# Turning the first block of a down projection with VectorE and GpSimd copies instead of TensorE

## The chip, the cores and the metric

The kernel runs on one core of one Trainium2 chip. A core has a matrix engine (TensorE, PE in the profile, with its weight loads as PEld), a vector engine (VectorE, DVE), a scalar engine (ScalarE, ACT), a general engine (GpSimd, POOL) and a queue engine that issues most loads (SyncE, SP). The metric is the device time of one execution in microseconds (us).

## The reference

A decoder trunk of two layers on 256 tokens of width 2048 in float32. Layer 0 mixes the tokens with gated linear attention, layer 1 with block-sparse attention; after each comes a convolutional feed-forward part:

```python
def conv_ffn(x, norm_w, w_up, conv_w, conv_b, w_down):
    h = rms_norm(x, norm_w) @ w_up
    hp = jnp.pad(h, ((0, 0), (CONV_WIDTH - 1, 0), (0, 0)))
    acc = conv_b
    for j in range(CONV_WIDTH):
        acc = acc + conv_w[j] * hp[:, j:j + S]
    a, u = jnp.split(acc, 2, axis=-1)
    return (jax.nn.silu(a) * u) @ w_down
```

and in the trunk `h = h + conv_ffn(h, ...)`. The hidden width is 5632. The change touches the end of layer 0's feed-forward: the product with `w_down`, its addition to `h`, and the first part of the norm that follows.

## The kernel before

*Layouts.* The residual `h` is kept with features on the 128 partitions and tokens along the free dimension: eight tiles `h[0]` to `h[7]`, each 128 x 2 x 256 (256 features). Two of them share one slot (`hs[m]`). The down projection's products come out the other way round, tokens on the partitions and features along the free dimension, so its result has to be turned before it is added to `h`.

*Precision.* A float32 product is made of three products of a reduced type: each weight tile of 1024 columns is split into `whi` (ACT copies, line 144) and `wlo` (DVE subtracts, line 146), and each activation likewise. Four buffers each hold `whi` and `wlo`. Raw weights come into three buffers `wraw` by DMAs on SP's queue, in a fixed order.

*The down projection* (`down`, line 766) works in two blocks of 1024 output features. A block goes through 22 pairs of hidden tiles (`hid[0]` to `hid[21]`) in an order that is written out by hand (`ORDERS`). For plain pairs it does 24 matmuls; for pairs marked `+` or `^` a Strassen-like scheme with seven products does 21, and uses sums of weights that were made earlier, parked in DRAM (`tsum`) and loaded back, for `+` into two buffers named `ahead`, for `^` into two slots named `sums`. Block 1 of layer 0 has the order `0 2 4 6 1+ 3+ 5+ 7+ 9+ 11+ 13+ 18 15^ 14+ 16+ 17^ 19+ 12^ 10+ 8^ 20 21`: four plain pairs, then almost only pairs with seven products. At the start of pair number i the jobs of entry i in a table are issued first; before pairs 8 and 10 of block 1 these include two combinations of hidden tiles (DVE and ACT work).

*Slots.* Large tiles (4 KB per partition) come from one pool of 32 slots, `slot(...)`. The 22 hidden tiles, the combinations (`comb`, 10 slots by the end of block 0), the tiles of `h` when loaded back, the norm's operands (`xw`) and the `sums` tiles all come from it. A tile whose slot is not free waits for the last reader of the old one.

*The work around the change* (`first_down`, line 902). Block 0 ends with four tiles of sums, 128 tokens x 512 features each (`blocks[0]`: two halves of the features, `c`, times two halves of the tokens, `t`). During block 1, for each quarter q from 0 to 3 of that block, `back(q, in_acc)` makes four TensorE transposes (line 921, against an identity) into half of a PSUM tile of the accumulators' pool, and DVE adds that to `h[q]` (line 923). `load_back(m)` (line 925) brings two tiles of `h` from DRAM, where they were parked, by DMAs on POOL's queue. `nrm.feed(q)` makes the next norm's operand (ACT line 258, DVE line 262) and its squares (ACT lines 269 and 272, DVE line 273). The second block's quarters, 4 to 7, are turned after block 1 by `last_back`, with TensorE into other PSUM banks.

*What sets the order.* Instructions are issued in program order by priority, but the order on each engine is laid out at compile time by a planner that goes by its own costs and by when data and buffers come free; each engine then works through its queue in order. `after_low()` keeps a DVE instruction behind the latest subtraction of weights (line 146) that was issued before it, `after_high()` the same on ACT.

*The turning by squares* exists already: in the up projection (`turn_up`, lines 720 and 722) DVE transposes all 32 x 32 squares of a 128 x 512 tile in place of each other (`V.transpose`), and `square` (line 705) moves the squares to their partitions with 16 POOL copies of 32 x 256 elements.

Of the kernel before, what the change touches and what calls it, by code (L numbers as in the profile page):

```python
# [8 lines left out]
F32 = mybir.dt.float32  # L9
# [9 lines left out]
S = 256  # L19
# [139 lines left out]
def trunk(ctx: ExitStack, tc: tile.TileContext, xT, cst, msk, w1p, w2a, w_k, w_qa, w_v2, w_v, w_g, w_go,  # L159
          w_up0, w_dn0, w_kk, w_kv, w_mq, w_mo, w_up1, w_dn1, rel, onehot, out):  # L160
    nc = tc.nc
    V, A, T = nc.vector, nc.scalar, nc.tensor
# [7 lines left out]
    acc_ps = ctx.enter_context(tc.tile_pool(name="acc_ps", bufs=3, space=PSUM))  # L170
# [3 lines left out]
    def slot(shape, dt, name):  # L174
        return big.tile(shape, dt, name=name, tag="slot")

    def temp(name, shape=(128, 2, S), dt=F32):
        return tmp.tile(list(shape), dt, name=name, tag="temp")

    def bank(name, shape):  # L180
        return mis_ps.tile(list(shape), F32, name=name, tag="bank")
# [6 lines left out]
    for layer, todo in enumerate(ahead):  # L188
        t = dram.tile([len(todo), 128, 2048], F32, name=f"tsum{layer}")
# [15 lines left out]
    h = [hs[p // 2][:, p % 2] for p in range(NP)]  # L205
# [44 lines left out]
    def col(c):  # L250
        return gn[:, c - C_GN:c - C_GN + 1] if C_GN <= c < C_GN + KT else cs[:, c:c + 1]
# [69 lines left out]
    def after(steps, job):  # L321
        later.append((cur[0] + steps, job))
# [21 lines left out]
    def after_high():  # L344
        return tc.issue_after(ws.high.ins)

    def after_low():
        return tc.issue_after(ws.low.ins)
# [40 lines left out]
    def rows(xs):  # L389
        return lambda kt: xs[kt // 2][:, kt % 2, :]  # L390

    def both(ps, name):
        t = temp(name)
        A.copy(t, ps[:, :, S:])
        V.tensor_add(t, t, ps[:, :, :S])
        return t
# [8 lines left out]
    def split(dst_hi, dst_lo, src):  # L405
        A.copy(dst_hi, src)
        V.tensor_sub(dst_lo, src, dst_hi.bitcast(F32))
# [23 lines left out]
    nrm = Norm(C_GN, "xw", columns=True)  # L431
# [12 lines left out]
    xs = rows(nrm.xs)  # L444
# [92 lines left out]
    for hd in range(GH):  # L537
# [4 lines left out]
        b = bcum[hd]  # L542
# [64 lines left out]
    for hd in range(GH):  # L607
        ps = gemm(xs, KT)
        q = both(ps, "q")
# [60 lines left out]
    def combine(k, hid_k, halves_, kept=True):  # L670

        own = room(k, hid_k, kept) if k not in combos else rooms_of[k]
        t = sums(halves_)
        if own is not None and not kept:
            return split(own[:, :, 0], own[:, :, 1], t)
        if own is not None:
            split(own[:, 0:3, 0], own[:, 0:3, 1], t[:, 0:3])
        else:
            for f in range(3):
                split(*combos[k][f], t[:, f])  # L680
        split(*combos[k][3], t[:, 3])
# [18 lines left out]
    def square(y, x):  # L700

        for m in range(4):
            xs_ = x[32 * m:32 * m + 32].rearrange("a t (n c b) -> a n t c b", c=4, b=32)
            for c in range(4):
                nc.gpsimd.tensor_copy(y[32 * c:32 * c + 32, :, :, 32 * m:32 * m + 32], xs_[:, :, :, c])  # L705

    def ffn(layer, nrm, then):
        xs = rows(nrm.xs)
        hid = []
        combos.clear()  # L710
        cw = C_CW + layer * 3 * 2 * FT
        cb = C_CB + layer * 2 * FT

        def turn_up(g, ps):

            x = slot([128, 2, 512], F32, "uT")
            us = [temp("up", (128, 512)) for _ in range(2)]
            for t in range(2):
                with after_high():
                    A.activation(us[t], ps[:, t, :], AF.Copy, scale=nrm.col[:, t:t + 1])  # L720
                with after_low():
                    V.transpose(x[:, t], us[t])  # L722
            y = slot([128, 2, 2, S], F32, "up")
            square(y.rearrange("p j i (t s) -> p (j i) t s", t=2), x)
            for jj in range(2):
                after(UP_LAG[jj], lambda jj=jj: conv(g, jj, y[:, jj]))

        def conv(g, jj, t):

            j = 2 * g + jj  # L730
            au = temp("au")
            for i in range(2):
                n = i * FT + j
                with after_high():
                    A.activation(au[:, i, :], t[:, i, :], AF.Identity, bias=col(cb + n),  # L735
                                 scale=col(cw + 2 * 2 * FT + n))
            for i in range(2):
                n = i * FT + j
                with after_low():
                    V.scalar_tensor_tensor(au[:, i, 1:], t[:, i, :S - 1], col(cw + 2 * FT + n), au[:, i, 1:],  # L740
                                           op0=OP.mult, op1=OP.add)
                V.scalar_tensor_tensor(au[:, i, 2:], t[:, i, :S - 2], col(cw + n), au[:, i, 2:],  # L742
                                       op0=OP.mult, op1=OP.add)
            after(1, lambda: gate(g, jj, au))

        def gate(g, jj, au):
            with after_high():
                A.activation(au[:, 0, :], au[:, 0, :], AF.Silu)
            with after_low():
                V.tensor_mul(au[:, 0, :], au[:, 0, :], au[:, 1, :])  # L750
            if jj == 0:
                hid.append(slot([128, 2, 2 * S], F32R, "hid"))
            split(hid[g][:, jj, :S], hid[g][:, jj, S:], au[:, 0, :])
            whole[jj] = (au[:, 0, :128], au[:, 0, 128:])
            if jj and (g in EARLY or g in ASIDE):
                two = [whole[0], whole[1]]
                after(1, lambda: combine(g, hid[g], two) if g in EARLY else put_aside(layer, g, hid[g], two))

        whole = {}

        for g in range(FT // 2):
            ps = gemm_tok(xs)
            after(0, lambda g=g, ps=ps: turn_up(g, ps))
        then(hid)
# [137 lines left out]
    def first_down(hid, nrm):  # L902
        blocks = {}

        def ready(b, p):
            blocks[b] = r = u_sums(p, None)

            def end(c, ns):
                for t, n in enumerate(ns):
                    V.tensor_add(r[2 * t + c], r[2 * t + c], p[n])  # L910

            return end

        def back(q, where):

            r = blocks[q // 4]
            tp = where()
            c, i0 = q % 4 // 2, q % 2 * 2
            for i in range(2):
                for t in range(2):  # L920
                    T.transpose(tp[:, i, 128 * t:128 * t + 128],
                                r[2 * t + c][:, 128 * (i0 + i):128 * (i0 + i) + 128], ident)
            V.tensor_add(h[q], h[q], tp)

        def load_back(m):
            hs[m] = slot([128, 2, 2, S], F32, "h")
            for q in (2 * m, 2 * m + 1):
                h[q] = hs[m][:, q % 2]
                nc.gpsimd.dma_start(h[q], hspill[q].rearrange("a (b c) -> a b c", b=2))

        pair = []

        def in_acc():
            if not pair:
                two = acc_ps.tile([128, 2, 512], F32, name="acc")
                pair.extend(two[:, i].rearrange("p (a b) -> p a b", a=2) for i in range(2))
            return pair.pop(0)

        jobs = {}
        for i, job, n in ((0, load_back, 0), (0, load_back, 1), (2, back, 0), (2, back, 1), (3, back, 2), (3, back, 3),  # L940
                          (4, nrm.feed, 0), (6, nrm.feed, 1), (8, nrm.feed, 2), (10, nrm.feed, 3),
                          (15, load_back, 2), (16, load_back, 3)):
            jobs.setdefault(i, []).append(lambda job=job, n=n: job(n, in_acc) if job is back else job(n))
        down(0, hid, ready, {1: jobs})

        def last_back(q):
            back(q, lambda: bank("hf", (128, 2, S)))
            nrm.feed(q)

        for q in range(4, NP):  # L950
            after(q - 3, lambda q=q: last_back(q))
        after(5, nrm.close)
# [3 lines left out]
    for p in range(NP):  # L956
        after(6 + 2 * p, lambda p=p: park(p))
    n_q = Norm(C_MN, "xw", rows=False, columns=True)
    ffn(0, n_ffn, lambda hid: first_down(hid, n_q))


# [79 lines left out]
    def turn(hd):  # L1041

        t = slot([128, 2, 384], F32, "pT")
        with tc.issue_after(ws.low.ins):
            V.transpose(t[:, 0], pts[hd])
        to = turned[hd].rearrange("f b (m a) -> m b f a", a=32)
        for m in range(4):
            nc.gpsimd.dma_start(to[m], t[32 * m:32 * m + 32, 0].rearrange("b (f a) -> b f a", a=32))
        nc.gpsimd.dma_start(t[:, 1].rearrange("k (j q) -> k j q", j=3),
                            turned[hd].rearrange("(j f) b q -> (f b) j q", f=4))  # L1050
        pts[hd] = t[:, 1]
# [26 lines left out]
    xs = rows(n_q.xs)  # L1078
# [10 lines left out]
    xs = rows(xkv)  # L1089
# [136 lines left out]
```

## Time and profile before

| | |
|---|---|
| median of three runs | 2176.6 us (2175.9 to 2176.62) |
| the profiled execution, its own time | 2175.2 us |
| its span in the trace | 2173.4 us |
| granted TensorE clock, mean | 1.00 |
| block 1 of the first down projection in the trace | about 976 to 1093 us |

The profile shows one execution. Busy time is given for each engine, with its share of the span. In lines of groups come the line of the code, the engine, the operation, the tile written and the tiles read, the shapes, the count, busy time and the mean duration in ns, then idle time of the engine before them and what ended it. In lines in order of time come the start and the length in us, and in brackets the idle time before and what released it. A window's line has, for each engine, busy time with the number of instructions, then the granted clock, the DMA engines' busy share and GB/s. A line of waits says who waited for whom: us in total, times, the longest.

### The profile page before, as it was taken

To read this page: it belongs to the slowest core of one execution; us is meant where nothing else is said; L and a number is where in the kernel's file an instruction comes from. 1 tells how busy PE (TensorE), PEld (TensorE's weight loads), DVE (VectorE), ACT (ScalarE), POOL (GpSimd) and SP (SyncE) were. 2 spreads that over 40 slices of the span, in tenths; PEclk is the share of its full clock that TensorE was granted. 3 is DMA by queue.
4 is the path that set the end of the run, shared out by engine and by line. 5 is a ranking of instruction groups with operands and counts; after the bars stand their busy time and mean duration, and the time that the engine had idled before them with its cause. 6 is when DMAs were issued, how large, how long until landed. Compare 5 with 4: busy or idle time off the path is not lost.

```text
span 2173.4 us, 29230 instructions
## 1 busy us (share of the span) xinstructions
PE 2165.5 (100%) x10224; PEld 1815.1 (84%) x10224; DVE 1829.8 (84%) x2531; ACT 1311.9 (60%) x1849; POOL 659.4 (30%) x925
## 2 busy tenths in 40 slices
PE   9999999999999999999999999999999999999999
PEld 7889888888888888887888888888888888888887
DVE  7676877699999897977978787677999999979898
ACT  6655655456565655766756666445565656567575
POOL 0000000264656464300001343003655565542000
PEclk9999999999999999999999999999999999999999
DMA  7575778777778785887967788677787878759896
GB/s 289 209 289 178 263 263 321 287 263 285 273 281 313 275 311 191 329 329 259 366 245 293 275 299 294 228 285 276 284 302 275 310 284 290 293 191 349 325 358 251
DMA packets 113526, 613.01 MB, mean 282 GB/s; under 512 B 29361, under 2 KB 29889, under 8 KB 49634
## 3 DMA queue, kind: packets, MB, share of 16 engines
q1 hardware_dynamic: 94610, 523.75, 66.5%
q0 software_dynamic: 18048, 86.60, 10.5%
q8 instruction: 80, 1.31, 0.2%
q10 hardware_dynamic: 720, 0.79, 0.1%
q14 instruction: 68, 0.56, 0.1%
HBM read 535.31 MB, written 75.78 MB: 281 GB/s over the span
## 4 chain that ended last, share of the span: by engine, by line
PE 98%; DMA 2%; DVE 0%; ACT 0%; issue 0%; ACTq 0%; DVEq 0%; SPq 0%
PE acc L381 40%; PE acc L384 20%; PE acc L803 13%; PE acc L366 11%; PE acc L368 6%; PE p L803 5%; DMA wraw<-w_dn 1%; PE sT L577 0%; DMA sums<-tsum 0%; DMA ahead<-tsum 0%; PE tr L1005 0%; PE s L1023 0%; DVE wlo L146 0%; DMA h<-xT 0%; PE z L483 0%; PE o L463 0%
## 5 line engine op out<-in xcount | busy, mean ns | idle before, releaser
L146 DVE TENSOR_TENSOR wlo<-wraw,whi 128x1024 fp32r<-128x1024 f32 (+1 forms) x788 | 954.3, 1221 | 266.6 <-ACT whi L144 179.8
L144 ACT CAST whi<-wraw 128x1024 fp32r<-128x1024 f32 (+1 forms) x788 | 797.1, 1018 | 611.9 <-PE acc L381 361.8
L381 PE MATMUL acc<-whi,xw 128*128 128x512 f32 x3328 | 825.5, 389 | 0.6 <-DVE xw L261 0.6
L381 PEld LDWEIGHTS acc<-whi,xw 128*128 128x128 f32 x3328 | 623.5, 188 | 130.4 <-issue 1.1
L705 POOL COPY up<-uT 32x256 f32<-32x256 f32 x704 | 520.9, 740 | 310.5 <-DVE uT L722 240.7
L384 PE MATMUL acc<-wlo,xw 128*128 128x512 f32 x1664 | 445.9, 389 | 0.0
L384 PEld LDWEIGHTS acc<-wlo,xw 128*128 128x128 f32 x1664 | 312.1, 188 | 65.0 <-DVE wlo L146 0.3
L339 POOL DMA_DIRECT2D tsum<-ahead x58 | 31.6, 545 | 549.3 <-DVE ahead L330 511.7
L803 PE MATMUL acc<-whi,hid 128*128 128x512 f32 x588 | 168.1, 390 | 1.3 <-ACT whi L144 1.3
L146 DVE TENSOR_TENSOR wlo<-ahead,whi 128x1024 fp32r<-128x1024 f32 x98 | 120.4, 1235 | 19.0 <-ACT whi L144 12.2
L803 PEld LDWEIGHTS acc<-whi,hid 128*128 128x128 f32 x588 | 109.8, 188 | 24.7 <-ACT whi L144 2.3
L381 PE MATMUL acc<-whi,xkv 128*128 128x512 f32 x512 | 129.9, 391 | 0.0
L144 ACT CAST whi<-ahead 128x1024 fp32r<-128x1024 f32 x98 | 101.9, 1054 | 42.9 <-PE p L803 18.5
L366 PE MATMUL acc<-xw,whi 128*128 128x512 f32 x512 | 124.5, 392 | 0.0
L803 PE MATMUL p<-whi,hid 128*128 128x512 f32 x356 | 111.5, 389 | 0.0
L381 PEld LDWEIGHTS acc<-whi,xkv 128*128 128x128 f32 x512 | 95.1, 188 | 18.9
L366 PEld LDWEIGHTS acc<-xw,whi 128*128 128x128 f32 x512 | 93.6, 188 | 17.7
L803 PE MATMUL acc<-whi,comb 128*128 128x512 f32 x348 | 101.3, 390 | 0.7 <-ACT whi L144 0.7
L803 PE MATMUL acc<-wlo,hid 128*128 128x512 f32 x294 | 96.3, 390 | 0.0
L735 ACT ACTIVATE au<-up,cs 128x256 f32<-128x256 f32 x176 | 96.1, 595 | 0.0
L742 DVE SCALAR_TENSOR_TENSOR au<-up,cs,au 128x254 f32<-128x254 f32 x176 | 90.2, 543 | 0.0
L740 DVE SCALAR_TENSOR_TENSOR au<-up,cs,au 128x255 f32<-128x255 f32 x176 | 89.2, 543 | 0.2
(266 smaller groups left out, 2355.3 us busy)
## 6 DMA issues: line engine op xcount, KB each, us to landing
wraw<-w_up SPq DMA_DIRECT2D x176, 1024.0 KB, 5.5
ahead<-w_dn SPq DMA_DIRECT2D x58, 1024.0 KB, 8.9
tsum<-ahead POOLq DMA_DIRECT2D x58, 1024.0 KB, 8.8
ahead<-tsum SPq DMA_DIRECT2D x49, 1024.0 KB, 6.9
wraw<-w_dn SPq DMA_DIRECT2D x58, 768.0 KB, 6.3
wraw<-w_dn SPq DMA_DIRECT2D x30, 1024.0 KB, 6.7
wraw<-w_g SPq DMA_DIRECT2D x16, 1024.0 KB, 4.9
wraw<-w_go SPq DMA_DIRECT2D x16, 1024.0 KB, 6.2
```

Source lines behind the costliest of these rows:

```text
L144: self.high = nc.scalar.copy(hi[:, a:b], src[:, a:b])
L146: self.low = nc.vector.tensor_sub(lo[:, a:b], src[:, a:b], hi[:, a:b].bitcast(F32))
L339: after(8, lambda: nc.gpsimd.dma_start(parked[layer][at], t))
L366: T.matmul(ps[:, b, :], two[i][0][:, c:c + 128], xs(kt), start=kt == 0, stop=False)
L368: T.matmul(ps[:, b, :S], two[i][1][:, c:c + 128], xs(kt)[:, :S], start=False, stop=kt == kts - 1)
L381: T.matmul(ps[:, t, :], xs(kt)[:, x0 + 128 * t:x0 + 128 * t + 128], hi[:, c:c + 512], start=kt == 0 and x0 == 0, stop=False)
L384: T.matmul(ps[:, t, :], xs(kt)[:, 128 * t:128 * t + 128], lo[:, c:c + 512], start=False, stop=kt == KT - 1)
L705: nc.gpsimd.tensor_copy(y[32 * c:32 * c + 32, :, :, 32 * m:32 * m + 32], xs_[:, :, :, c])
L735: A.activation(au[:, i, :], t[:, i, :], AF.Identity, bias=col(cb + n), scale=col(cw + 2 * 2 * FT + n))
L740: V.scalar_tensor_tensor(au[:, i, 1:], t[:, i, :S - 1], col(cw + 2 * FT + n), au[:, i, 1:], op0=OP.mult, op1=OP.add)
L742: V.scalar_tensor_tensor(au[:, i, 2:], t[:, i, :S - 2], col(cw + n), au[:, i, 2:], op0=OP.mult, op1=OP.add)
L803: T.matmul(p[n], x[xi], w[wi][:, 512 * f:512 * f + 512], start=n not in begun, stop=left[n] == 0)
```

## The change

Block 0's four tiles of sums are no longer turned by TensorE. `turn(c)` (at pairs 1 and 3 of block 1) takes the two token halves of feature half c, has DVE transpose their 32 x 32 squares into a slot, and POOL move the squares into a second slot with 16 copies. `join(q)` (at pairs 4, 5, 8 and 9) adds a quarter of that to `h[q]` on DVE, both inputs in SBUF. The feeds of the norm for quarters 0 to 3 move from pairs 4, 6, 8 and 10 to pairs 6, 7, 10 and 11. The two PSUM tiles of `in_acc` are gone. Block 1's own quarters (`last_back`) are turned as before.

```diff
+    def squares(name, xs):
+
+        x, y = slot([128, 2, 512], F32, name + "T"), slot([128, 4, S], F32, name)
+        for t in range(2):
+            with after_low():
+                V.transpose(x[:, t], xs[t])
+        square(y.rearrange("p n (t s) -> p n t s", t=2), x)
+        return y
+
...
-        def back(q, where):
+        turned_ = {}
+
+        def turn(c):
+            turned_[c] = squares("hf", [blocks[0][2 * t + c] for t in range(2)])
+
+        def join(q):
+            y = turned_[q // 2]
+            with after_low():
+                V.tensor_add(h[q], h[q], y[:, q % 2 * 2:q % 2 * 2 + 2])
+
+        def back(q):
 
             r = blocks[q // 4]
-            tp = where()
+            tp = bank("hf", (128, 2, S))
...
-        pair = []
-
-        def in_acc():
-            if not pair:
-                two = acc_ps.tile([128, 2, 512], F32, name="acc")
-                pair.extend(two[:, i].rearrange("p (a b) -> p a b", a=2) for i in range(2))
-            return pair.pop(0)
-
         jobs = {}
-        for i, job, n in ((0, load_back, 0), (0, load_back, 1), (2, back, 0), (2, back, 1), (3, back, 2), (3, back, 3),
-                          (4, nrm.feed, 0), (6, nrm.feed, 1), (8, nrm.feed, 2), (10, nrm.feed, 3),
+        for i, job, n in ((0, load_back, 0), (0, load_back, 1), (1, turn, 0), (3, turn, 1),
+                          (4, join, 0), (5, join, 1), (6, nrm.feed, 0), (7, nrm.feed, 1),
+                          (8, join, 2), (9, join, 3), (10, nrm.feed, 2), (11, nrm.feed, 3),
                           (15, load_back, 2), (16, load_back, 3)):
-            jobs.setdefault(i, []).append(lambda job=job, n=n: job(n, in_acc) if job is back else job(n))
+            jobs.setdefault(i, []).append(lambda job=job, n=n: job(n))
         down(0, hid, ready, {1: jobs})
 
         def last_back(q):
-            back(q, lambda: bank("hf", (128, 2, S)))
+            back(q)
             nrm.feed(q)
```

The function `square`, which `squares` calls, is unchanged:

```python
def square(y, x):
    for m in range(4):
        xs_ = x[32 * m:32 * m + 32].rearrange("a t (n c b) -> a n t c b", c=4, b=32)
        for c in range(4):
            nc.gpsimd.tensor_copy(y[32 * c:32 * c + 32, :, :, 32 * m:32 * m + 32], xs_[:, :, :, c])
```

## The prediction

> **What bounds the kernel now.** I read the first page of the profile for the engines, then the view by windows for the stage that the change touches, then the waits and the order of time inside it.
>
> ```profile
> span 2173.4 us, 29230 instructions
> PE 2165.5 (100%) x10224; PEld 1815.1 (84%) x10224; DVE 1829.8 (84%) x2531; ACT 1311.9 (60%) x1849; POOL 659.4 (30%) x925
> PE 98%; DMA 2%; DVE 0%; ACT 0%; issue 0%; ACTq 0%; DVEq 0%; SPq 0%
> ```
>
> TensorE (PE) works all the time and the chain of what ended last is 98% PE, so a microsecond of PE work taken away is a microsecond saved, as long as weights still arrive. The windows from the start of block 1 of the first down projection onward show where that holds.
>
> ```profile
> core 0: us, PE busy (x) PEld busy (x) DVE busy (x) ACT busy (x) POOL busy (x), PEclk, DMA share, GB/s
> 978.00:1000.00 22.00, 22.00 (x104) 18.16 (x103) 14.73 (x18) 12.11 (x16) 2.15 (x4) 1.00 0.54 194
> 1000.00:1020.00 20.00, 20.00 (x92) 16.58 (x90) 16.96 (x20) 13.73 (x18) 0.00 (x0) 1.00 0.80 282
> 1020.00:1045.00 25.00, 24.20 (x103) 18.51 (x102) 23.78 (x35) 19.69 (x27) 0.00 (x0) 1.00 0.98 377
> 1045.00:1078.00 33.00, 33.00 (x148) 27.32 (x147) 29.37 (x29) 24.86 (x28) 2.15 (x4) 1.00 0.97 379
> ```
>
> Up to 1000 us (four plain pairs) VectorE (DVE) idles 22 - 14.73 = 7.3 us. From 1000 on the pairs are those with seven products, and DVE idles 20 - 16.96 = 3.0, then 25 - 23.78 = 1.2, then 33 - 29.37 = 3.6 us. The third window is the only one where PE falls short of full, and what it waits for is the split of the weights:
>
> ```profile
> PEld acc L803 <- ACT whi L144: 1.5, 2, 0.8
> PEld acc L803 <- DVE wlo L146: 1.3, 4, 0.6
> PEld p L803 <- ACT whi L144: 0.2, 1, 0.2
> 1020.70 0.76 PEld L803 LDWEIGHTS acc<-whi,comb 128*128 128x128 f32 x4 [0.75 <-ACT whi L144]
> 1033.45 0.30 PEld L803 LDWEIGHTS acc<-wlo,comb 128*128 128x128 f32 x2 [0.28 <-DVE wlo L146]
> ```
>
> All the waits between 975 and 1135 us are these 1.5 + 1.3 + 0.2 = 3.0 us; the two rows of the order of time are the first and the last of seven, all between 1020 and 1034. So this stretch is already bound by DVE and by the weights that follow it, not by PE. How DVE holds the weights is in the chain:
>
> ```profile
> 1010.73 1.24 DVE wlo L146
> 1011.99 7.51 DMA ahead<-tsum
> 1019.59 1.06 ACT whi L144
> ```
>
> A load into one of the two "ahead" buffers starts when DVE has finished the subtraction that reads the old one, takes 7.5 us, then ScalarE (ACT) and DVE split it. A late DVE makes the next load late.
>
> **The change, part by part.** The sum is made against the profiled execution, 2175.2 us (span 2173.4 and 1.8 around it); the median of the runs, 2176.6, is 1.4 above it.
>
> *Removed from PE:* 16 transposes and the PSUM tiles that they fill.
>
> ```profile
> 981.52 0.22 PE acc L921 x2
> 987.22 0.22 PE acc L921 x2
> 992.67 0.44 PE acc L921 x4
> 993.34 0.44 PE acc L921 x4
> 1000.16 0.44 PE acc L921 x4
> ```
>
> 0.22 + 0.22 + 3 x 0.44 = 1.76 us of the chain, weight loads hidden within. All lie where PE waits for nothing, so this comes off in full: -1.8.
>
> *DVE, additions.* Before, four additions from PSUM:
>
> ```profile
> 987.48 0.69 DVE L923 TENSOR_TENSOR h<-h,acc 128x512 f32<-128x512 f32 x1 [1.30 <-PE acc L921]
> 994.88 0.68 DVE L923 TENSOR_TENSOR h<-h,acc 128x512 f32<-128x512 f32 x1
> 995.48 0.88 DVE L262 SCALAR_TENSOR_TENSOR xw<-h,cs,xw 128x256 fp32r<-128x256 f32 x2
> 996.27 0.69 DVE L273 TENSOR_TENSOR acc_sq<-acc_sq,hsq 128x512 f32<-128x512 f32 x1
> 998.01 0.69 DVE L273 TENSOR_TENSOR acc_sq<-acc_sq,hsq 128x512 f32<-128x512 f32 x1
> 1001.46 0.68 DVE L923 TENSOR_TENSOR h<-h,acc 128x512 f32<-128x512 f32 x1
> ```
>
> An addition costs 0.60 from start to start (994.88 to 995.48). Three lay before 1000, where DVE has 7 us to spare. The change puts four of the same size at pairs 4, 5, 8 and 9, after 1000: +4 x 0.60 - 0.60 = +1.8 us in the tight stretch. The feeds of the norm must follow them, so the operand at 995.48 (0.8) and the two sums of squares (2 x 0.6), done before 1000 now, move in as well: +2.0. Feeds at 1000 and later stay in the stretch either way.
>
> *DVE, squares.* Two turns of two transposes each, and 16 copies on GpSimd (POOL) per turn. The same pair of operations runs in the up projection:
>
> ```profile
> 650.47 1.30 DVE L722 STREAM_TRANSPOSE uT<-up 128x512 f32<-128x512 f32 x2
> 651.90 12.65 POOL L705 COPY up<-uT 32x256 f32<-32x256 f32 x16 [4.57 <-DVE uT L722]
> ```
>
> So 1.3 us of DVE and 12.65 us of POOL per turn. Per copy that is 0.79 us. The Trainium skill (GPSIMD Engine Reference, section Engine selection) calls one-input work on GpSimd "roughly line-rate"; with its 1.03 cycles an element at 1.2 GHz the 16 copies would take an estimated 3.5 us and no join could be late. The row decides against it.
>
> When the turns run is set by the pool of 32 slots, each turn needing two. The 22 hidden tiles and 10 rooms of combinations hold all of them when block 1 begins, and the loads of h show how they come free:
>
> ```profile
> 981.82 1.08 POOL L929 DMA_DIRECT2D h<-hspill  x2 [94.73 <-PE p L803]
> 987.52 1.07 POOL L929 DMA_DIRECT2D h<-hspill  x2 [4.61 <-PE acc L921]
> 993.38 0.92 ACT L258 ACTIVATE xw<-h,cs 128x256 fp32r<-128x256 f32 x2 [0.25 <-PE p L803]
> ```
>
> One slot per finished pair: h at 982 and 987.5, an operand at 993.4. With the change the third goes to the transposed tile of turn 0, the fourth (end of pair 3, about 998) to its square; copies then run to about 1010, and turn 1 follows with the slots of pairs 4 and 5, copying to about 1023. So turn 1's transposes land after 1000: +1.3. Turn 0's lie in the 7.3 us of room and cost nothing; if that room were gone they would cost 1.3 too.
>
> *DVE beside POOL.* The subtraction of 1024 columns by form, first between 651.9 and 664.5, while POOL copies, then between 1004 and 1020, while it rests; then the first stretch as a window:
>
> ```profile
> L146 DVE TENSOR_TENSOR wlo<-wraw,whi 128x1024 fp32r<-128x1024 f32 x4 | 5.7, 1416 | 0.0
> L146 DVE TENSOR_TENSOR wlo<-wraw,whi 128x1024 fp32r<-128x1024 f32 x3 | 3.7, 1219 | 0.0
> 651.90:664.50 12.60, 12.60 (x58) 10.42 (x57) 12.17 (x16) 6.10 (x8) 11.98 (x16) 1.00 0.76 301
> ```
>
> 1416 against 1219 ns: DVE does 14% less per microsecond while POOL copies. Over 2 x 12.65 = 25.3 us at DVE's share here, (16.96 + 23.78) / 45 = 91%, that is 25.3 x 0.91 x 0.14 = 3.2 us.
>
> *POOL's queue.* Its only other work in block 1 is the issue of loads of h; the last two pairs' loads are due at pairs 15 and 16, after the copies. Nothing: but if the copies ran past 1045, those loads would be behind them, with half of the norm's last feeds behind these.
>
> *Sum.* DVE in 1000 to 1045 gets 1.8 + 2.0 + 1.3 + 3.2 = 8.3 us more and has 3.0 + 1.2 = 4.2 idle: 4.1 over. In this stretch PE already stands for DVE's lateness, so I take the whole of it as PE time: +4.1 - 1.8 = +2.3. Ends: if feeds are put off until the next window, its 3.6 us of idle help and 0.5 remains, -1.3; if none of the idle can be used, because DVE idles there for weights that have not landed, +8.3 - 1.8 = +6.5. I take the middle since PE's waits lie exactly where DVE idles least. 2175.2 + 2.3 = 2177.5 profiled, 2178.9 as a median.
>
> **Rivals.**
>
> *A: the joins stand in DVE's queue and wait for POOL* (slower). If the planned order has the first join at its pair (4, about 998 to 1003) though the copies end at 1010.5, DVE stands with the weight subtractions queued behind it, and PE waits for these. Four buffers of split weights allow three halves of 4.76 / 4 = 1.19 us, less 1.06 for ACT and 1.22 for DVE: 1.3 us of cover. From about 999.5 PE would lose 1010.5 - 999.5 - 1.3 = 9.7 us; the pause gives DVE room for the rest, so +9.7 - 1.8 = +7.9, a median of 2184.5. It decides from the point where DVE comes to a join more than 1.3 us before its last copy ends. For it: DVE does stand for POOL in one other place,
>
> ```profile
> DVE q L997 <- POOL rr L995: 2.4, 2, 1.9
> ```
>
> against it: feeds in the rows above run when their data are ready rather than at their pair, so the order seems made with some idea of durations.
>
> *B: the slots run short for the weights* (slower). Later pairs take parked sums into two slots by the loading queue (SP):
>
> ```profile
> 1026.83 0.90 SPq L120 DMA_DIRECT2D sums<-tsum  x2
> ```
>
> Four more slots are out until the copies and joins are done (about 1010 and 1023 to 1027). If that load waits for one more pair, all weight loads behind it on SP wait too: 4.76 us on top of the sum, a median near 2183.7. Against it: both transposed tiles and the first square are back by about 1023.
>
> *C: the saving stays* (faster side). Feeds fill idle time, and PE keeps its 1.8 us, perhaps with part of the 3.0 us of waits: -1.8 to -4.8, a median of 2174.8 down to 2171.8. For it: the norm is wanted only after block 1, so the added DVE work can wait.
>
> *D: the port is a lock.* If copies and two-input DVE work could not overlap at all, 25.3 us of copies would meet 4.2 us of idle: +25.3 - 4.2 - 1.8 = +19, a median of 2196. The Trainium skill (SBUF — State Buffer, section on the two separate sides) states this rule: the loser of the shared pair "fully blocks". The window above disagrees: DVE is busy 12.17 and POOL 11.98 of 12.6 us at once.
>
> **How the numbers follow.** 0.2% of 2176.6 is 4.4 us, about what a measurement of this kernel can tell from no change. Chances: the sum 0.54 (0.43 within 0.2%, 0.11 slower, by its upper end), A 0.22, B 0.11, C 0.11 (0.07 within, 0.04 faster), D 0.02. Together: faster 0.04, same 0.50, slower 0.46. The forecast is the sum's, 2178.9; its own range is 2175.3 to 2183.1. The range reaches up to take in A and B whole and some way into C: 2173.5 to 2187.0, leaving out D, the deep end of C and a worse A.
>
> **What would show it.** No PE rows of the transposing line among block 1's pairs, and 1.76 us less PE work there; copies of 12 to 13 us each, the first starting about 998; the subtractions between 998 and 1023 at 1.4 us; PE's waits in the stage grown from 3.0 to about 7 us, at DVE's subtractions; no long wait of DVE on POOL (A) and none of SP at the sums (B). It is wrong if DVE waits for POOL by several microseconds, if PE's waits don't grow, or if the copies run early, before the seven-product pairs.

## The result and the profile after

The changed kernel takes 2178.51 us (median of 20 runs), the one before 2175.96 us (20 runs on the same chip): a ratio of 1.0012, with a 95% interval of 1.0006 to 1.0017. So it is about 2.6 us slower, between 1.3 and 3.7: clear of zero, and within 0.2%. The profiled execution took 2179.16 us.

The first page of the changed kernel's profile:

```profile
span 2177.3 us, 29235 instructions
PE 2166.5 (100%) x10208; PEld 1814.2 (83%) x10208; DVE 1837.1 (84%) x2535; ACT 1308.5 (60%) x1849; POOL 686.3 (32%) x957
```

PE has 16 instructions less, DVE 7.3 us of work more, POOL 27 us more. The windows over the stretches from 978 to 1045 (columns: busy us and instructions of PE, PEld, DVE, ACT, POOL, then granted clock, DMA share, GB/s):

```profile
978.00:1000.00 22.00, 22.00 (x99) 18.22 (x98) 13.68 (x14) 10.16 (x11) 4.23 (x7) 1.00 0.54 192
1000.00:1020.00 20.00, 19.91 (x88) 15.94 (x86) 19.63 (x19) 14.16 (x18) 19.19 (x20) 1.00 0.84 303
1020.00:1045.00 25.00, 22.13 (x85) 16.64 (x86) 25.00 (x36) 18.29 (x26) 6.85 (x11) 0.93 0.90 333
```

Of the 4.2 us that DVE idled between 1000 and 1045, 0.4 are left, all of it before 1000.5; from then on DVE has no pause up to 1045. PE falls short in the third window by 2.9 us instead of 0.8.

How long block 1 takes can be read on PE. It runs from a group of eight matmuls that both kernels have at its start (at 974.56 us before, at 974.48 after) to the first transposition of the quarters that stay with TensorE, before and after:

```profile
1093.42 0.27 PE L921 MATMUL hf<-mk,c 128*128 128x128 f32 x1
1096.08 0.27 PE L940 MATMUL hf<-mk,c 128*128 128x128 f32 x1
```

That is 118.9 and 121.6 us: block 1 alone is 2.7 us longer, so the loss is where the change is. The waits of PE's weight loads from 960 to 1135 us:

```profile
PEld acc L812 <- DVE wlo L146: 3.5, 4, 1.4
PEld acc L812 <- ACT whi L144: 2.1, 5, 0.8
PEld p L812 <- ACT whi L144: 1.0, 1, 1.0
```

6.6 us where there were 3.0, and just over half, 3.5 us, now stands at DVE's subtraction, 1.3 before. In order of time, the first of them and the longest:

```profile
1018.24 0.77 PEld L812 LDWEIGHTS acc<-whi,comb 128*128 128x128 f32 x4 [0.27 <-ACT whi L144]
1027.06 0.19 PEld L812 LDWEIGHTS acc<-wlo,hid 128*128 128x128 f32 x1 [1.41 <-DVE wlo L146]
```

Seven waits, 5.8 us in all, lie between 1018 and 1030; the other 0.8 are three short ones after 1071. What the engines did there, first POOL's queue in order of time:

```profile
987.18 1.06 POOL L948 DMA_DIRECT2D h<-hspill  x2 [4.36 <-PE p L812]
997.83 29.43 POOL L705 COPY hf<-hfT 32x256 f32<-32x256 f32 x32 [9.59 <-PE p L812]
```

The copies of both turns begin at 997.8 and end at 1027.3, without a pause. DVE's joins in order of time:

```profile
1015.89 1.69 DVE L931 TENSOR_TENSOR h<-h,hf 128x512 f32<-128x512 f32 x2
1035.41 1.28 DVE L931 TENSOR_TENSOR h<-h,hf 128x512 f32<-128x512 f32 x2
```

They have no idle time before them: the order has them behind the data. And DVE's subtraction by form, from 998 to 1027 (count, then busy us and mean ns):

```profile
L146 DVE TENSOR_TENSOR wlo<-ahead,whi 128x1024 fp32r<-128x1024 f32 x9 | 12.2, 1372 | 1.5 <-ACT whi L144 1.5
L146 DVE TENSOR_TENSOR wlo<-wraw,whi 128x1024 fp32r<-128x1024 f32 x5 | 7.0, 1410 | 0.4 <-ACT whi L144 0.4
L146 DVE TENSOR_TENSOR wlo<-wraw,whi 128x512 fp32r<-128x512 f32 x5 | 4.4, 879 | 0.0
```

with, in the kernel before, over the same time:

```profile
L146 DVE TENSOR_TENSOR wlo<-wraw,whi 128x512 fp32r<-128x512 f32 x5 | 3.4, 686 | 0.0
```

The subtractions of 1024 columns take 1372 to 1410 ns beside the copies, where 1219 to 1223 was the undisturbed figure; those of 512 columns take 879 instead of 686. The longer time is nearly the same for both, 0.15 to 0.19 us for each instruction. The copies, one by one (shortest, median and longest, in ns):

```profile
L705 POOL COPY hf<-hfT x32: 388/764/1402, 997.8 to 1026.5; 32x256 f32<-32x256 f32 x32
```

All 32 move the same amount, and yet they last from 0.39 to 1.40 us. Why is told in the last section.

### The profile page after: what moved, and what is told of

Its sections match the earlier page's. It is cut to its first block, busy times and chain, and to the rows that moved or that the text cites. A ratio compares the mean times of both kernels' runs of the same rounds, so it can differ in the third digit from the quotient of the medians.

```text
span 2177.3 us, 29235 instructions
## 1 busy us (share of the span) xinstructions
PE 2166.5 (100%) x10208; PEld 1814.2 (83%) x10208; DVE 1837.1 (84%) x2535; ACT 1308.5 (60%) x1849; POOL 686.3 (32%) x957
## 4 chain that ended last, share of the span: by engine, by line
PE 51%; DMA 1%; DVE 0%; ACT 0%; issue 0%; SPq 0%; ACTq 0%
PE acc L381 23%; PE acc L384 11%; PE acc L812 9%; PE p L812 3%; PE acc L366 3%; PE acc L368 1%; DMA wraw<-w_dn 1%; DMA sums<-tsum 0%; PE tr L1017 0%; PE s L1035 0%; DVE wlo L146 0%; PE o L463 0%; PE s L1033 0%; ACT whi L144 0%; PE o L461 0%; PE o L460 0%
## 5 line engine op out<-in xcount | busy, mean ns | idle before, releaser
L144 ACT CAST whi<-wraw 128x1024 fp32r<-128x1024 f32 (+1 forms) x788 | 795.8, 1016 | 624.7 <-PE acc L381 368.9
```

What stands on the lines that cost most here:

```text
L144: self.high = nc.scalar.copy(hi[:, a:b], src[:, a:b])
```

## The experiments

The theory is that of the sum: PE pays for what VectorE is given to do among the pairs with seven products, part of it through GpSimd's copies. Its rivals are that the place of the feeds and joins makes the loss, that copies beside VectorE cost nothing, and that slots and the weights' loads set the time. Waits are those of PE's weight loads from 960 to 1135 us in one profile; ratios are to the kernel before on the same chip, with the 95% interval; us are the ratio's difference from one, times 2176 (differences of medians lie within 1.1 us of these). The last column is how much longer block 1 is than in the kernel before, read on PE as above, in the one profiled execution. It leaves out what varies elsewhere: the rest of the program takes between 2054.2 and 2057.5 us by the same reading in all of them but two (2060.9 with turns first, 2052.8 for the changed kernel with late combinations). How much block 1 itself varies from one execution to the next is not known.

| kernel | ratio, interval | us | waits, us | block 1, us |
|---|---|---|---|---|
| before | 1 | 0 | 3.0 | 0 |
| changed | 1.0012, 1.0006 to 1.0017 | +2.6 | 6.6 | +2.7 |
| no turning | 0.9985, 0.9976 to 0.9994 | -3.3 | 0.7 | -4.8 |
| no copies | 0.9998, 0.9990 to 1.0007 | -0.4 | 4.1 | -0.6 |
| before with 32 copies | 1.0007, 0.9998 to 1.0016 | +1.5 | 4.8 | +1.6 |
| before with 64 copies | 1.0022, 1.0012 to 1.0032 | +4.8 | 7.3 | +4.0 |
| before with moved feeds | 1.0007, 0.9998 to 1.0016 | +1.5 | 2.6 | 0.0 |
| turns first | 1.0038, 1.0025 to 1.0050 | +8.3 | 9.9 | +6.7 |
| turns first, loads by SP | 1.0005, 0.9996 to 1.0014 | +1.1 | 4.4 | -0.2 |
| joins on GpSimd | 1.0043, 1.0030 to 1.0055 | +9.4 | 12.0 | +7.8 |
| late joins | 1.0011, 1.0002 to 1.0020 | +2.4 | 8.4 | +2.8 |
| before, late combinations | 0.9991, 0.9982 to 0.9999 | -2.0 | 3.1 | +0.7 |
| changed, late combinations | 1.0020, 1.0011 to 1.0029 | +4.4 | 9.7 | +6.2 |
| turns first, loads by SP, late combinations | 1.0004, 0.9995 to 1.0013 | +0.9 | 6.1 | +1.8 |

### No turning at all

```diff
-                          (0, load_back, 0), (0, load_back, 1), (1, turn, 0), (3, turn, 1),
-                          (4, join, 0), (5, join, 1), (6, nrm.feed, 0), (7, nrm.feed, 1),
-                          (8, join, 2), (9, join, 3), (10, nrm.feed, 2), (11, nrm.feed, 3),
+                          (0, load_back, 0), (0, load_back, 1),
+                          (6, nrm.feed, 0), (7, nrm.feed, 1),
+                          (10, nrm.feed, 2), (11, nrm.feed, 3),
```

> Leaves out the turning of block 0's sums and their addition to h (half of the first feed-forward's result is missing), nothing else of the changed kernel: no transposes on PE or DVE, no copies, no joins, the feeds at pairs 6, 7, 10, 11. The theory of the sum (DVE is overloaded among the seven-product pairs and PE pays) expects PE's 1.8 us to stay saved and the waits to fall back to the 3 us of before or less: 1.8 to 3.5 us below the kernel before. A theory that the moved feeds alone make the loss expects it to stay near the changed kernel, 1 to 2.5 us above the kernel before.

It is 3.3 us faster than the kernel before, where 1.8 us of transposes and 2.3 us of waits, 4.1 together, come off the path; block 1 is 4.8 us shorter. The moved feeds are in this kernel too, so they alone don't make the loss. The waits that are left:

```profile
PEld acc L812 <- ACT whi L144: 0.7, 2, 0.5
```

A window of it:

```profile
1020.00:1045.00 25.00, 24.98 (x110) 20.11 (x109) 25.00 (x39) 20.22 (x29) 1.07 (x2) 1.00 0.99 383
```

Its DVE is busy all of these 25 us, more than in the kernel before (23.78), and PE hardly waits: a full DVE alone does not make waits. Then its first two reloads of the "ahead" buffers after 999, on SP's queue in order of time:

```profile
999.38 0.33 SPq L106 DMA_DIRECT2D ahead<-tsum  x1
1004.60 0.33 SPq L106 DMA_DIRECT2D ahead<-tsum  x1
```

and the same view of the kernel before:

```profile
1000.78 0.33 SPq L106 DMA_DIRECT2D ahead<-tsum  x1
1007.46 0.33 SPq L106 DMA_DIRECT2D ahead<-tsum  x1
```

The second reload comes 5.2 us after the first here and 6.7 us there, where an addition and operands of the norm stand among the subtractions. So part of the 3.0 us before may be a lateness that began near 1003 and was paid from 1020 on, by the weights that went through this buffer. From 1000 to 1020 this kernel moves 331 GB/s and the kernel before 282; after that the transfer engines are busy 0.99 and 0.98 of the time, so there is little room to catch up. That reading fits both traces; no run delays this one reload by itself.

### Transposes and joins without copies

```diff
-        x, y = slot([128, 2, 512], F32, name + "T"), slot([128, 4, S], F32, name)
+        x = slot([128, 2, 512], F32, name + "T")
...
-        square(y.rearrange("p n (t s) -> p n t s", t=2), x)
-        return y
+        return x.rearrange("p t (n s) -> p (t n) s", n=2)
```

> The changed kernel without GpSimd's 32 copies: the joins add the tile that VectorE transposed, whose 32 x 32 squares are not in their places (so block 0's sums are added in a wrong order), and each turn takes one slot instead of two. The sum without its 3.2 us for DVE beside POOL, and with the turns no later than 1000 us: DVE gets about 4 us more against 4.2 of idle, so PE's waits grow by 0 to 1 us and the kernel is 0.8 to 1.8 us below the one before. If the slowing beside POOL does not matter and the joins and moved feeds make the loss, it stays 1 to 2.5 us above the one before.

0.4 us below the kernel before and not told apart from it; the waits of 4.1 us are more than expected, 0 to 1 us above 3.0. Against no turning, transposes and joins (with the feeds tied to them) come to 2.9 us; against the changed kernel, the copies come to 3.0 us. Each of these two differences carries more than 2 us of uncertainty (two intervals of about ±2 and ±1.2 to ±2 us), so the second was tried directly. By the length of block 1 they are 4.2 and 3.3 us. Leaving the copies out also sets a slot free and lets the joins run early, so the second is not the copies' work on DVE alone.

### The copies alone, once and twice

```diff
+        spare = []
+
+        def copies(c):
+            if not spare:
+                spare.append(slot([128, 4, S], F32, "spare"))
+            square(spare[0].rearrange("p n (t s) -> p n t s", t=2), hid[20].bitcast(F32))
...
-        for i, job, n in ((0, load_back, 0), (0, load_back, 1), (2, back, 0), (2, back, 1), (3, back, 2), (3, back, 3),
+        for i, job, n in ((0, load_back, 0), (0, load_back, 1), (1, copies, 0), (3, copies, 1), (2, back, 0), (2, back, 1), (3, back, 2), (3, back, 3),
```

> The kernel before with nothing taken away and the 32 copies added on GpSimd at pairs 1 and 3, from a hidden tile into one spare slot that nobody reads. The sum expects only the slowing of VectorE, 3.2 us among the seven-product pairs less what idle time takes: 1 to 3 us above the kernel before, with the subtractions at 1.4 us while the copies run. If copies beside VectorE cost PE nothing, as in the up projection, 0; if they make the whole loss of the change (2.5 measured and 1.8 saved), 4.3.

The 1.5 us have zero in their interval; block 1 is 1.6 us longer. The dose was doubled, with `(5, copies, 2), (7, copies, 3)` put in as well:

> The kernel before with 64 copies on GpSimd that nobody reads, twice those of the earlier try, at pairs 1, 3, 5 and 7, so that they run until about 1050 us, through the stretch where PE waits. If VectorE's slowing beside them is paid by PE there, 50 us of it take 50 x 0.9 x 0.14 = 6.4 us of VectorE's time, of which idle time takes up to 4: 2 to 6 us above the kernel before, and at least twice the loss of 32 copies. If the 1 us measured with 32 copies is chance: level.

4.8 us, clear of zero. POOL's queue in this kernel with 64 copies:

```profile
993.17 65.29 POOL L705 COPY spare<-hid 32x256 f32<-32x256 f32 x64 [4.82 <-PE p L803]
```

Its third window:

```profile
1020.00:1045.00 25.00, 22.87 (x96) 17.31 (x95) 25.00 (x30) 17.44 (x24) 23.66 (x24) 1.00 0.90 349
```

The waits, and the subtraction by form from 998 to 1045:

```profile
PEld acc L803 <- DVE wlo L146: 5.9, 8, 1.7
PEld acc L803 <- ACT whi L144: 1.4, 2, 0.9
```

```profile
L146 DVE TENSOR_TENSOR wlo<-wraw,whi 128x1024 fp32r<-128x1024 f32 x9 | 12.5, 1392 | 0.0
```

Nothing reads these copies and nothing waits for them. They cost time through DVE: no idle time left, 1392 ns for the subtraction, and waits that were 1.3 us at DVE's output grown to 5.9. The slot that the spare tile takes is not the reason: SP waits 3.2 us at the parked sums from 975 to 1094, as in the kernel before. Twice the copies cost about three times as much by the middles, as it would be if the first 32 had still met idle time; the intervals are too wide to show that.

### The feeds alone

```diff
-                          (4, nrm.feed, 0), (6, nrm.feed, 1), (8, nrm.feed, 2), (10, nrm.feed, 3),
+                          (6, nrm.feed, 0), (7, nrm.feed, 1), (10, nrm.feed, 2), (11, nrm.feed, 3),
```

> The kernel before with only the four feeds moved to the pairs of the changed kernel (6, 7, 10, 11 for 4, 6, 8, 10). The sum counts 2.0 us of vector work moving in among the seven-product pairs, which 4.2 us of idle time there can take: 0 to 1 us above the kernel before. If the place of the feeds alone makes the loss, 2.5 or more.

1.5 us above, with zero in the interval, and waits of 2.6 us: the profile shows no loss from the feeds' place, and block 1 is as long as before.

### The turns earlier

```diff
-        for i, job, n in ((0, load_back, 0), (0, load_back, 1), (1, turn, 0), (3, turn, 1),
+        for i, job, n in ((0, turn, 0), (1, turn, 1), (2, load_back, 0), (3, load_back, 1),
```

> The changed kernel with the two turns issued at pairs 0 and 1, ahead of the loads of h, which go to pairs 2 and 3; so the turns take the first slots that come free. If the slots set the time of the turns, the first copies start near 987 us instead of 998 and all of them end near 1013 instead of 1027; by the sum that takes about half of the 3.2 us and all of the turns' 1.3 us out of the seven-product pairs: 2.5 - 1.6 - 1.3, from 1.5 below to 0.5 above the kernel before. If the place of the joins and feeds makes the loss, no gain on the changed kernel (2.5 above).

A clear miss, 8.3 us slower. POOL's queue in this kernel:

```profile
988.50 10.00 POOL L705 COPY hf<-hfT 32x256 f32<-32x256 f32 x16 [99.95 <-PE p L812]
999.38 17.40 POOL L705 COPY hf<-hfT 32x256 f32<-32x256 f32 x16 [0.88 <-PE p L812]
1016.73 2.13 POOL L948 DMA_DIRECT2D h<-hspill  x4
```

The copies begin 9 us earlier, as foreseen (they end at 1016.8, not at 1013): the slots do set the time of the turns. But the loads of h stand behind them on POOL's queue until 1016.7, joins come late and slots stay occupied. SP's queue, at the parked sums:

```profile
1042.26 9.90 SPq L120 DMA_DIRECT2D sums<-tsum  x6
```

These loads began at 1026.8 before. PE's longest wait follows:

```profile
1049.25 1.36 PEld L812 LDWEIGHTS acc<-whi,comb 128*128 128x128 f32 x4 [6.87 <-ACT whi L144]
```

To tell the queue from the early turns, the loads of h went to SP's queue, at pairs 3 and 4:

```diff
-                nc.gpsimd.dma_start(h[q], hspill[q].rearrange("a (b c) -> a b c", b=2))
+                (nc.sync if m < 2 else nc.gpsimd).dma_start(h[q], hspill[q].rearrange("a (b c) -> a b c", b=2))
...
-        for i, job, n in ((0, load_back, 0), (0, load_back, 1), (1, turn, 0), (3, turn, 1),
-                          (4, join, 0), (5, join, 1), (6, nrm.feed, 0), (7, nrm.feed, 1),
+        for i, job, n in ((0, turn, 0), (1, turn, 1), (3, load_back, 0), (4, load_back, 1),
+                          (5, join, 0), (5, join, 1), (6, nrm.feed, 0), (7, nrm.feed, 1),
```

> The turns at pairs 0 and 1 once more, ahead of the loads of h, but these loads go by SP's queue at pairs 3 and 4 instead of GpSimd's, where they stood behind the copies until 1017 us. If that queue (and the slots held for so long) was the loss of the earlier try, and the sum holds, the joins run by about 1010 and 1018 and the kernel is from 1.5 below to 0.5 above the kernel before. If the turns before the loads are bad in themselves, because SP waits for slots with the weights behind it, it stays 4 us or more above.

The 8 us are gone: 1.1 above the kernel before and not told apart from it, nor from the changed kernel, by its middle a little over what was expected. Block 1 is as long as before, within 0.2 us. POOL's queue for the second turn:

```profile
997.71 15.27 POOL L705 COPY hf<-hfT 32x256 f32<-32x256 f32 x16 [0.88 <-PE p L812]
```

and the waits:

```profile
PEld acc L812 <- ACT whi L144: 2.5, 4, 1.3
PEld acc L812 <- DVE wlo L146: 1.9, 2, 1.0
```

The copies end at 1013 instead of 1027, the first turn's while DVE has room, and the waits are 4.4 us instead of 6.6. So early turns aren't bad in themselves; the loads behind them were (with the loads and the first join one pair later, which this edit moves too).

### The joins on GpSimd, or later

```diff
-            with after_low():
-                V.tensor_add(h[q], h[q], y[:, q % 2 * 2:q % 2 * 2 + 2])
+            nc.gpsimd.tensor_add(h[q], h[q], y[:, q % 2 * 2:q % 2 * 2 + 2])
```

> The changed kernel with the four joins done by GpSimd behind its copies instead of by VectorE. If VectorE's time among the seven-product pairs is what PE pays for, 4 x 0.60 to 0.80 us less on it, less about 0.6 for the longer work beside GpSimd, gives 1.5 to 2.5 us below the changed kernel, level with the kernel before. If it is only the slowing beside GpSimd that costs, GpSimd's additional work makes it 0 to 1 us slower than the changed kernel.

Another miss, 9.4 us slower. GpSimd's joins in order of time:

```profile
1029.45 7.98 POOL L930 TENSOR_TENSOR h<-h,hf 128x512 f32<-128x512 f32 x4
```

Four additions take 8.0 us where DVE would take 2.4, all behind the last copy, to 1037.4. SP's loads of the parked sums slip to 1040.7, and PE waits 7.4 us in one piece at 1041. The join became the end of a longer chain that holds slots. Nor was VectorE's time saved: its subtractions beside these additions took up to 2.3 us instead of 1.2. Putting the joins off on DVE instead:

```diff
-                          (4, join, 0), (5, join, 1), (6, nrm.feed, 0), (7, nrm.feed, 1),
-                          (8, join, 2), (9, join, 3), (10, nrm.feed, 2), (11, nrm.feed, 3),
+                          (11, join, 0), (11, join, 1), (11, nrm.feed, 0), (12, nrm.feed, 1),
+                          (12, join, 2), (13, join, 3), (13, nrm.feed, 2), (14, nrm.feed, 3),
```

> The changed kernel with joins and feeds put off to pairs 11 to 14 (pair 11 is a plain one). If the overload from 1015 to 1035 us is what costs, about 5 us of vector work leaves it, half of it meets idle time later, and the kernel is 1 to 2.5 us below the changed one. If instead the slots are what is short (the squares hold theirs longer, and SP waits for the slots of the parked sums), it is slower than the changed kernel, by up to a pair, 4.8 us.

2.4 us above the kernel before, not told apart from the changed one: a miss too. Its waits are 4.2 us up to 1031 and 4.2 us again from 1048 on: the load on DVE was moved along and met no idle time there that PE didn't pay for.

### Other work out of the same stretch

Two combinations of hidden tiles are made before pairs 8 and 10. They were put off to pairs 11 and 14, in the kernel before, in the changed one, and in the one with early turns and loads by SP:

```diff
-MADE = {5: 0, 17: (1, 4), 7: 1, 9: 2, 11: 3, 19: (4, 4), 13: 5, 15: 6, 16: 7, 12: 9, 14: 11, 10: 8, 8: 10, 18: 6, 6: 4}
+MADE = {5: 0, 17: (1, 4), 7: 1, 9: 2, 11: 3, 19: (4, 4), 13: 5, 15: 6, 16: 7, 12: 9, 14: 11, 10: 11, 8: 14, 18: 6, 6: 4}
```

> The kernel before with only the two combinations moved to pairs 11 and 14. By the overload of VectorE, up to the 3.0 us of waits go: 1 to 3 us below the kernel before. If the waits come from the weights' own loads: level.

> The changed kernel with only the two combinations moved to pairs 11 and 14. By the overload of VectorE, 4.1 us of its work leave the stretch where the copies and joins run and meet about 2 us of overload later: 1 to 3 us below the changed kernel, level with the kernel before. If only the copies, joins and transposes themselves matter: no change from the changed kernel, 2.5 above.

> The variant with early turns and the loads of h on SP's queue, and in addition the two combinations of hidden tiles (2.1 us of vector work each) made at pairs 11 and 14 instead of 8 and 10, in both layers. If any vector work taken out of 1015 to 1035 us gives PE that time, its 4.4 us of waits shrink to 1 to 2 and the kernel is 1.5 to 3 us below the kernel before, the first that beats both. If the waits come from the weights' own loads, no change from the variant without it (0.5 above).

The kernel before gained 2.0 us (0.2 to 3.9): the fastest kernel here that does all the work, and the only one that beats both, though by an interval that barely leaves zero out among thirteen such comparisons. Its third window:

```profile
1020.00:1045.00 25.00, 23.37 (x102) 18.36 (x101) 20.97 (x27) 18.15 (x23) 0.00 (x0) 1.00 0.96 368
```

DVE idles 4.0 us in it, and yet PE waits 3.1 us in the stage. Its longest wait:

```profile
1027.53 0.77 PEld L803 LDWEIGHTS acc<-whi,comb 128*128 128x128 f32 x4 [2.05 <-ACT whi L144]
```

and what the chain has ahead of that:

```profile
1016.96 9.37 DMA ahead<-tsum
```

So here PE waits beside an idle DVE, for weights that land late, 9.4 us after their buffer came free. But the edit moved loads, too. Two loads of parked sums that began together at 1026.83 in the kernel before begin here at

```profile
1010.88 0.33 SPq L120 DMA_DIRECT2D sums<-tsum  x1
1015.64 0.32 SPq L120 DMA_DIRECT2D sums<-tsum  x1
```

right ahead of that reload, which may be why it took 9.4 us and not 7.5. So this run does not tell what PE waits for in the kernel before. That kernel's own trace has both kinds. The first of its waits, 0.75 us at 1020.70, ends the reload of 7.5 us in the prediction's chain, and DVE waits there as well:

```profile
1020.68 1.22 DVE L146 TENSOR_TENSOR wlo<-ahead,whi 128x1024 fp32r<-128x1024 f32 x1 [2.22 <-ACT whi L144]
```

From there DVE has no pause until 1044, and the 1.3 us of waits at its output lie in that stretch. With the late combinations none of these 1.3 us is left. The number came out as expected and the mechanism did not: the waits are as long as before, block 1 is 0.7 us longer, and the profiled execution (2175.61 us) is no faster than that of the kernel before. Where the 2 us came from stays open; the edit also moves combinations in layer 1.

The changed kernel got no better by the same edit, and by its middle worse, where 1 to 3 us of gain were expected. It has a new wait:

```profile
1069.71 0.50 PEld L812 LDWEIGHTS acc<-whi,comb 128*128 128x128 f32 x2 [3.44 <-ACT whi L144]
```

behind, in its chain, a load of parked sums that began at 1056.5, only when a late combination had been made, and took 11.8 us. Its waits up to 1033 fell only from 5.8 to 4.9 us. With early turns the edit changed nothing that could be told in the time, and the waits are 6.1 us where 1 to 2 were expected.

## Why the prediction was right, and where it was not

Forecast 2178.9 us, measured 2178.5; +2.3 us against +2.6. Step by step:

- *PE's 1.8 us* came off: PE has its 16 transposes less, and without the new work the kernel is 3.3 us faster than before (with part of the waits in it; no run takes off the 1.8 alone).
- *The turns' place* was right: the first copy at 997.8, foreseen about 998, for the reason given (the slots after the two loads of h). The copies took 29.4 us in all, not 25.3, and ended at 1027, not 1023. The row used came from the up projection; here DVE had no pause, and each copy waits for DVE's instruction.
- *DVE beside POOL*, 3.2 us, is a step that failed in its mechanism: "DVE does 14% less per microsecond while POOL copies". The loss is not a share of the time but 0.13 to 0.23 us for each DVE instruction with two inputs, long or short. The row of 1024 columns came as foreseen (1410 ns, 1416 assumed), but the many shorter instructions lose more. Summed by form over 998 to 1027, against the same forms in the kernel before, DVE is busy an estimated 5.0 us longer. That it costs time is shown by the 64 copies that nobody waits for.
- *Transposes, joins and feeds*, 1.3 + 1.8 + 2.0 of DVE's time: turn 1's transposes did land after 1000, and the feeds behind the joins. Their joint cost to the whole, against no such work, is 2.9 us.
- *The idle time.* The sum let DVE use up its 4.2 us, and it did, but for 0.4. PE's waits grew by 3.6 us, 4.1 foreseen, 2.2 of them at DVE's subtractions and not all. Neither end of that term came true.
- *Why PE waits before the change* was half right: "In this stretch PE already stands for DVE's lateness". Of the 3.0 us, 1.3 stand at DVE's output while DVE has no pause; at least the first wait, 0.75 us, is for weights that landed late. What starts that lateness stays open.
- *The number* is partly luck. With 5.0 in the place of 3.2 the same sum gives +4.1, above the interval of the measurement (1.3 to 3.7). So not all of DVE's added work became PE's time, and the two errors nearly cancel.
- *Rival A* did not happen. All that DVE waited for in the changed kernel between 975 and 1094:

```profile
DVE wlo L146 <- ACT whi L144: 13.1, 11, 3.6
DVE hfT L712 <- PE p L812: 2.0, 1, 2.0
DVE wlo L146 <- PE p L812: 1.7, 2, 1.4
DVE c L919 <- PE p L812: 0.2, 1, 0.2
```

GpSimd is not among it: the joins were ordered behind their copies, at 1016 and 1035, not at their pairs.

- *Rival B* was there without its price. SP's wait at the parked sums, in the same stretch:

```profile
SPq L120 <- PE p L812: 4.7, 2, 2.7
```

It was 1.7 us at this row before. But after 1030 PE has only the 0.8 us at 1071 to 1073. The mechanism is real where the slots come back later: with turns first and with joins on GpSimd it made one wait of 7 us.

- *Rival C* needs work that costs nothing when put off; late joins showed none.
- *Rival D*: the lock is there, and its price was not. The prediction put it out by both engines being busy at once (12.17 and 11.98 of 12.6 us), but an instruction that stands for the other engine counts as busy. The rows of single copies, in the last section, show each engine waiting for the other's instruction, as rival D has it. The +19 us took the 25.3 us for the copies' own time; a copy that meets no two-input work takes 0.43 us from start to start, 32 of them 14 us, and DVE's loss is the 5.0 us above.

## What to carry to other kernels

Work taken off a busy matrix engine is a gain only if the engines that feed it can carry what takes its place: 1.8 us of transposes were paid for with vector work and with copies on an engine that looked free, some 3 us each (both with over 2 us of uncertainty). Price an idle engine by what it does to its neighbour, instruction by instruction, and a moved job by its whole chain: the queue it stands in, the buffers it holds and the loads that it moves. Busy time can hide waiting, so look at the shortest and the longest of equal instructions. A wait at the vector engine's output can have begun earlier, so move one job, and see what else moved with it, before the place of a wait is taken for its cause.

## What the hardware showed unexpectedly

*The matrix engine's clock.* Three short windows of the changed kernel's profiled execution (the column before the last two is the granted clock):

```profile
1028.00:1030.00 2.00, 1.22 (x4) 0.77 (x4) 2.00 (x4) 1.05 (x1) 0.00 (x0) 0.79 0.45 105
1030.00:1032.00 2.00, 2.00 (x6) 1.52 (x6) 2.00 (x3) 1.46 (x2) 0.00 (x0) 0.50 0.93 351
1032.00:1034.00 2.00, 2.00 (x9) 1.62 (x8) 2.00 (x4) 0.94 (x1) 0.00 (x0) 0.86 0.74 242
```

The clock is halved for about 0.42 + 1 + 0.28 windows, 3.4 us, some 1.7 us of PE's work, from within the last of the seven waits of 5.8 us in all. None of these is longer than 1.4 us. The Trainium skill (TensorE: Matmul & The Clock Gate, section A second HAM failure mode: psum-queue depth-cycling) tells of such a clock falling through frequent short idling, in a kernel that cycles through PSUM; this trace agrees on the idling, with the numbers just given, and here PE idles for weights. It is not what made the change slower: 3 of its 20 executions have a mean clock below 1 (0.999), and the other 17 have a median of 2178.44 us. The kernel before has it in 16 of 94 executions beside the experiments, which took 1.2 to 2.2 us longer by their medians than the others on the same chip. A mean below 1 does not tell where: in the profiles with 32 and 64 copies the half clock lies near 2140 us, in layer 1. Where PE waits 7 us in one piece it comes each time: all five executions of the kernel with turns first have a mean clock of 0.997 or 0.998, and so have all five with joins on GpSimd. With the 3.4 us wait of the changed kernel with late combinations it is below 1 in 10 of 11. A window after the wait of 6.9 us with turns first:

```profile
1049.20:1054.00 4.80, 4.75 (x11) 3.79 (x12) 4.80 (x7) 3.54 (x5) 0.00 (x0) 0.50 0.77 276
```

4.75 us at half clock are up to 2.4 us lost on top of the wait; the half clock lasts until about 1054.7, which makes it up to 2.7. So a wait of that size can cost some 40% more than itself.

*VectorE and GpSimd wait for each other's instruction.* In the kernel with turns first, seven copies began while DVE did nothing but two transposes, of one input each:

```profile
992.38 3.01 POOL L705 COPY hf<-hfT 32x256 f32<-32x256 f32 x7
```

That is 0.43 us from one to the next, and the two transposes took their usual 1.30 us. Beside subtractions, which have two inputs, the same copies last longer by the length of what they meet: about 1.3 us beside one of 1024 columns and 0.76 beside one of 512, so 16 of them took 14.7 us beside a full DVE. In return each such instruction of DVE waits for the copy that is running and is longer by 0.13 to 0.23 us, whatever its own length. A two-input addition on GpSimd shows it more strongly:

```profile
L930 POOL TENSOR_TENSOR h<-h,hf x4: 1259/2272/2287, 1029.5 to 1035.2; 128x512 f32<-128x512 f32 x4
1031.72 2.32 DVE L146 TENSOR_TENSOR wlo<-ahead,whi 128x1024 fp32r<-128x1024 f32 x1
```

The shortest of the four took 1.26 us, the others 2.3, and a subtraction beside them 2.32 us instead of 1.22. The Trainium skill (GPSIMD Engine Reference, section 4.1 Engine selection) puts two-input work at about twice VectorE's time; the shortest agrees, against 0.60 to 0.69 us on DVE.
